# An instruction planner with measured waits, half-width prices and the exclusion of two engines

## The chip, the cores and the metric

The kernel runs on one core of a Trainium2 chip. The metric is the device time of one execution in microseconds (us). The kernel before took 1173.47 us, the median of three runs between 1171.46 and 1174.13.

## The reference

Two layers act on 1024 tokens of width 1024, in float32. Each layer normalises its input, projects it with one matrix into the inputs of four groups of heads and a gate, runs the groups, normalises each group, multiplies by the gate, projects back and adds the normalised result to its input:

```python
h = rmsnorm(x, g_pre) @ w_in
ya = swa_sink_attention(a_q, a_k, a_v, sinks)        # A: window of 128, softmax
yb = short_gated_conv(b_b, b_c, b_x, conv_w, conv_b) # B: gated convolution
yc = mla(c_q, c_kv, c_kr, pos, ...)                  # C: causal softmax, low-rank q and kv
yd = stick_breaking_attention(d_q, d_k, d_v)         # D: sigmoid breaks
y = concat of rmsnorm(group) * silu(gate)
x = x + rmsnorm(y @ w_out, g_post)
```

In group D the weight of key j for query i is sigmoid(z_ij) times the product of 1 - sigmoid(z_ik) over the keys k between them.

## The kernel before

**Engines and precision.** All large products are matmuls on TensorE (PE). A float32 operand is held as two halves, a rounded high part and the rest; most products take three matmuls (high by high, high by low, low by high). Making the halves, a *split*, takes a cast on ScalarE (ACT) for the high part and a subtraction on VectorE (DVE) or GpSimd (POOL) for the low part. Most splits read the accumulator in PSUM and run on VectorE. Those of weights read SBUF and may run on either engine.

**Tiles.** xg are the long-lived tiles (34 buffers), xw the weights' splits and also the name of the projection's two accumulator banks, xP six tiles of attention weights (128 queries by up to 1024 keys), xsc three banks of scores, xtr two banks of transposes, xpv the one bank of the values' product, xPT the split of transposed attention weights, xf tiles of the gate, xt small temporaries.

**Group D.** A task takes one head and 256 queries, as two blocks of 128. For each block the scores go through two sigmoids on ScalarE, then VectorE runs the cumulative product, a `tensor_tensor_scan` of 128 x w with w up to 1024, and a multiply of 128 x (w - 1), both in place in xP tiles. The following task step `pv_causal` transposes the blocks on TensorE into xtr, splits them into xPT (ScalarE the cast, VectorE the subtraction), and multiplies them with the values into xpv. The trace's operation TENSOR_TENSOR_SCAN is printed in the order as SCALAR_TENSOR_TENSOR of xP with xP. The four heads come as two pairs; the scores of the first pair are D0, of the second D1.

**What sets the order.** No order is written by hand. The work is a set of streams (Python generators: norms, projections, scores, value products, gates, output). A planner, the class `Weaver`, runs them while the program is built, and keeps a clock of its own: `now` for TensorE and a list of busy stretches for each of VectorE, ScalarE, GpSimd and the DMA queue. Whenever TensorE is free by that clock, `run` takes the first stream whose operands are ready by it, or else the one ready soonest. Every instruction of the other engines is issued through one call in the class `Tracked` (line 85, so all of them carry L85 in the trace). `enter` computes when an instruction's operands are ready, with a latency from the table `LAT` by the engine that made them and the engine that reads (P TensorE, V VectorE, A ScalarE, G GpSimd, D DMA, S a scan), and how long it takes; `place` puts it in the first gap of its engine that is long enough. The order on each engine is then pinned as the planner's clock has it, so it stays the same on the chip, while the instants do not: an instruction waits for its real operands. `sooner` decides between GpSimd and VectorE for the splits of weights, with 300 ns added against VectorE.

**What the change cannot alter.** The projection stream takes two banks in turn; its tiles for group A's keys wait until the last scores of D1 have been recorded. `matmul` (L479) and `transpose` (L483) carry the names xw, xsc, xpv and xtr of the bank that they fill.

## Time and profile before

| | us |
|---|---|
| median of three runs | 1173.47 |
| the profiled execution | 1172.81 |
| its span, first to last instruction | 1171.0 |
| PE busy | 1142.7 |
| DVE busy | 822.9 |
| ACT busy | 640.1 |
| POOL busy | 347.9 |

Each layer repeats the same sequence: the input norm and the projections for C and B, the attention of C, the stage of group D (255 to 400 us and 832 to 977 us of the span), then groups A, the gates and the output projection. TensorE is close to always busy, so the idle stretches of TensorE and what ended them are the first thing to read. A bracket at a row's end, [2.10 <-DVE xPT L85], is the idle time before its instructions and the instruction that ended it. PEclk is the granted clock of TensorE as a share of 2.4 GHz. Busy time of a matmul is longer than the distance between two starts, since matmuls overlap: the distance is what counts in a sum.

### The profile page before, as it was taken

What the parts mean: (1) busy time and instruction counts of PE and PEld (TensorE: products, weight loads), DVE (VectorE), ACT (ScalarE), POOL (GpSimd) and SP (SyncE); (2) the same over time, 40 slices, a digit from 0 to 9 for tenths busy, and PEclk for the clock granted to TensorE, in tenths of its full rate; (3) what the DMA queues carried; (4) which work ended last, traced back from release to release, by engine and by line L of the source; (5) the groups of instructions that cost most, each with busy time, mean ns of one, the idle gap of its engine ahead of it and who ended that gap; (6) DMA issues with size and microseconds to landing.
All of it is one profiled execution on the core that took longest, in us unless ns stands there. A gap on an engine that the chain in (4) does not pass through costs nothing.

```text
span 1171.0 us, 17883 instructions
## 1 busy us (share of the span) xinstructions
PE 1142.7 (98%) x6302; PEld 978.2 (84%) x6302; DVE 822.9 (70%) x1685; ACT 640.1 (55%) x1443; POOL 347.9 (30%) x477
## 2 busy tenths in 40 slices
PE   8999999999999999999999999999999999999997
PEld 6988888987787788878889888899878877888886
DVE  6868687549969878852764777873688788888323
ACT  7665566246556667631454655651655565675211
POOL 4225143116224235310221332420353332451000
PEclk9999999999999999999999999999999999999999
DMA  6121202121111011321451122021201111124123
GB/s 227 36 64 33 68 19 60 50 81 27 27 37 37 18 37 52 98 73 46 161 166 29 37 54 55 19 82 36 76 25 37 27 28 28 28 64 155 61 72 126
DMA packets 72678, 71.98 MB, mean 61 GB/s; under 512 B 10062, under 2 KB 59276, under 8 KB 72588
## 3 DMA queue, kind: packets, MB, share of 16 engines
q1 hardware_dynamic: 72588, 70.83, 20.4%
q8 instruction: 50, 0.82, 0.3%
q14 instruction: 40, 0.33, 0.1%
HBM read 55.09 MB, written 11.53 MB: 57 GB/s over the span
## 4 chain that ended last, share of the span: by engine, by line
PE 73%; DVE 14%; ACT 5%; issue 4%; DMA 2%; POOL 1%; SPq 0%; DVEq 0%; POOLq 0%; ACTq 0%
PE xw L479 37%; PE xsc L479 22%; PE xtr L483 8%; DVE xP L85 7%; PE xpv L479 6%; DVE xg L85 3%; ACT xP L85 2%; DMA xP<-in_w_out_dram 1%; DVE xPT L85 1%; ACT xg L85 1%; DVE xs L85 1%; ACT xt L85 1%; DVE xt L85 1%; POOL xs L85 1%; DVE xw L85 1%
## 5 line engine op out<-in xcount | busy, mean ns | idle before, releaser
L479 PE MATMUL xw<-xg,xw 128*128 128x512 f32 x2064 | 516.7, 396 | 2.4 <-DVE xf L85 2.4
L479 PEld LDWEIGHTS xw<-xg,xw 128*128 128x128 f32 x2064 | 376.0, 188 | 75.3 <-DVE xf L85 3.3
L479 PE MATMUL xsc<-xg,xg 128*128 128x512 f32 (+7 forms) x1400 | 307.2, 364 | 0.3 <-ACT xP L85 0.2
L479 PEld LDWEIGHTS xsc<-xg,xg 128*128 128x128 f32 (+1 forms) x1400 | 239.0, 190 | 37.6 <-ACT xP L85 4.1
L85 POOL TENSOR_SCALAR xP<-xP,xs 128x256 f32<-128x256 f32 (+7 forms) x128 | 82.5, 656 | 161.7 <-DVE xs L85 113.5
L85 ACT CAST xPT<-xtr 128x512 fp32r<-128x512 f32 (+1 forms) x192 | 101.2, 550 | 49.7 <-PE xtr L483 48.1
L479 PE MATMUL xpv<-xPT,xg 128*128 128x256 f32 (+1 forms) x720 | 120.2, 290 | 7.0 <-DVE xPT L85 6.5
L483 PE MATMUL xtr<-ident,xP 128*128 128x128 f32 (+1 forms) x843 | 124.3, 275 | 2.7 <-DVE xP L85 1.5
L85 DVE TENSOR_TENSOR xPT<-xtr,xPT 128x512 fp32r<-128x512 f32 (+1 forms) x192 | 117.0, 630 | 11.3 <-ACT xPT L85 10.9
L479 PEld LDWEIGHTS xpv<-xPT,xg 128*128 128x128 f32 x720 | 103.2, 189 | 23.9 <-DVE xPT L85 13.6
L479 PE MATMUL xw<-xg,xg 128*128 128x416 f32 (+2 forms) x648 | 114.5, 326 | 0.0
L85 DVE TENSOR_TENSOR xg<-xw,xg 64x512 fp32r<-64x512 f32 (+1 forms) x112 | 62.9, 574 | 69.7 <-ACT xg L85 68.5
L85 ACT CAST xg<-xw 64x512 fp32r<-64x512 f32 (+1 forms) x112 | 53.4, 492 | 103.0 <-PE xw L479 92.5
L483 PEld LDWEIGHTS xtr<-ident,xP 128*128 128x128 f32 (+1 forms) x843 | 97.7, 141 | 14.2 <-DVE xP L85 3.5
L85 ACT ACTIVATE xP<-xP,xs 128x256 f32<-128x256 f32 (+7 forms) x128 | 80.7, 631 | 49.0 <-DVE xs L85 43.8
L85 POOL TENSOR_TENSOR xw<-xraw,xw 128x512 fp32r<-128x512 f32 x42 | 64.8, 1546 | 139.2 <-ACT xw L85 102.7
L479 PEld LDWEIGHTS xw<-xg,xg 128*128 128x128 f32 x648 | 102.0, 189 | 1.9
L85 DVE TENSOR_TENSOR_SCAN xP<-xP 128x128 f32<-128x128 f32 (+3 forms) x64 | 95.3, 1488 | 4.3 <-ACT xP L85 4.2
L85 POOL TENSOR_TENSOR xt<-xt 64x128 f32<-64x128 f32 x64 | 40.0, 626 | 153.1 <-DVE xt L85 124.6
L85 ACT ACTIVATE xP<-xsc 128x512 f32<-128x512 f32 (+2 forms) x192 | 80.1, 514 | 9.2 <-DVE xP L85 8.1
L85 ACT ACTIVATE xt<-xsc 128x512 f32<-128x512 f32 x32 | 19.2, 599 | 116.4 <-PE xsc L479 92.6
L85 ACT COPY xt<-xpv 64x512 f32<-64x512 f32 x80 | 46.7, 584 | 44.7 <-PE xpv L479 43.4
(128 smaller groups left out, 1291.9 us busy)
## 6 DMA issues: line engine op xcount, KB each, us to landing
xraw<-in_w_in_dram SPq DMA_DIRECT2D x96, 256.0 KB, 2.8
xP<-in_w_out_dram SPq DMA_DIRECT2D x16, 512.0 KB, 3.9
xg<-in_x_dram SPq DMA_DIRECT2D x8, 512.0 KB, 9.0
xg<-xP SPq DMA_DIRECT2D x32, 128.0 KB, 2.3
xP<-in_x_dram SPq DMA_DIRECT2D x8, 512.0 KB, 4.2
xP<-xs SPq DMA_DIRECT2D x8, 512.0 KB, 3.8
xs<-xP SPq DMA_DIRECT2D x7, 512.0 KB, 3.5
out_dram<-xP SPq DMA_DIRECT2D x7, 512.0 KB, 2.6
```

Of the source, the lines that this page charges most:

```text
L85: ins = real(*args, **kw)
L479: in_order(T.matmul(ps, lhs, rhs, start=start, stop=stop, skip_group_check=True))
L483: in_order(T.transpose(ps, src, idn))
```

## The change

It changes the planner's prices; no line that issues work is touched.

- The table of latencies takes new numbers (ScalarE to TensorE 250 to 165 ns, VectorE to TensorE 195 to 140, VectorE to VectorE 60 to 115, GpSimd to TensorE 190 to 60, a new one of 110 for ScalarE to ScalarE, and others).
- An instruction of at most 64 partitions and at least 128 elements is priced 125 ns more on ScalarE and 95 ns more on VectorE. `tensor_reduce` is priced 117 ns more.
- The factor 1.12 on VectorE's `tensor_tensor` between SBUF operands goes; the price of GpSimd's goes from 2.5 to 2.25 ns an element.
- `place` gets a flag `pair`. It is set for VectorE's scans, its `tensor_tensor` with SBUF operands, its `tensor_scalar` with SBUF operands, and GpSimd's `tensor_tensor`, all with at least 128 elements. Such an instruction may not start by the planner's clock while one of the other engine's is running. It is not set for GpSimd's `tensor_scalar` or VectorE's `scalar_tensor_tensor`. `sooner` asks with the flag set.

```diff
 LAT = {
-    "PA": 197, "PV": 197, "AV": 90, "AP": 250, "AG": 160, "VP": 195, "VA": 128, "VG": 155,
+    "PA": 198, "PV": 200, "AV": 137, "AP": 165, "AG": 177, "VP": 140, "VA": 128, "VG": 165,
...
-    def place(self, key, t, dur, keep=True):
+    def place(self, key, t, dur, keep=True, pair=False):
         busy = self.busy[key]
-        i = len(busy)
-        while i > 0 and busy[i - 1][1] > t:
-            i -= 1
-        while i < len(busy) and busy[i][0] < t + dur:
-            t = max(t, busy[i][1])
-            i += 1
+        other = self.port["G" if key == "V" else "V"] if pair else ()
+        while True:
+            i = len(busy)
+            while i > 0 and busy[i - 1][1] > t:
+                i -= 1
+            while i < len(busy) and busy[i][0] < t + dur:
+                t = max(t, busy[i][1])
+                i += 1
+            end = max([e for s, e in other if s <= t < e], default=t)
+            if end <= t:
+                break
+            t = end
         if not keep:
             return t
+        if pair:
+            self.port[key] = self.port[key][-40:] + [(t, t + dur)]
...
+        pair = False
+        half = out.shape[0] <= 64 and n >= 128
         if key == "A":
...
+            dur += 125.0 * half
...
         elif key == "V":
-            half = op == "tensor_scalar" and not bank
-            dur = 69.0 + (0.52 if half else 1.04) * n + 62.0 * scalars
+            fast = op == "tensor_scalar" and not bank
+            dur = 69.0 + (0.52 if fast else 1.04) * n + 62.0 * scalars + 95.0 * half
+            pair = (fast or op == "tensor_tensor") and not bank and n >= 128
             if op == "tensor_tensor_scan":
                 dur = 110.0 + 2.12 * n
-            elif op == "tensor_tensor" and not bank:
-                dur *= 1.12
+                pair = True
+            elif op == "tensor_reduce":
+                dur += 117.0
...
         elif op == "tensor_scalar":
             dur = 244.0 + 0.833 * n
         else:
-            dur = 148.0 + 2.5 * n
+            dur = 148.0 + 2.25 * n
+            pair = n >= 128
...
-        t = self.place(key, t, dur)
+        t = self.place(key, t, dur, pair=pair)
...
-            dur = 148.0 + 2.5 * n if e.key == "G" else 69.0 + 1.04 * n
-            t = self.place(e.key, t, dur, False) + dur + (300.0 if e.key == "V" else 0.0)
+            dur = 148.0 + 2.25 * n if e.key == "G" else 69.0 + 1.04 * n
+            t = self.place(e.key, t, dur, False, True) + dur + (300.0 if e.key == "V" else 0.0)
```

The sets of instructions on TensorE, ScalarE and the DMA queue stay the same; three splits in all move from VectorE to GpSimd, as a balance of moves both ways. What moves is the order. Three places of the first layer follow; the second layer has the same. Numbers behind names differ between the two programs, so the same tile has two numbers.

VectorE, second head pair of D, before: the splits of a task's transposes, the scans and multiplies of the next one (blocks of 896 and 1024 keys), and at the end the task's last split, of 384 columns.

```order
L85 TENSOR_TENSOR xPT_4299<-xtr_4294,xPT_4299 128x512
L85 TENSOR_TENSOR xPT_4314<-xtr_4309,xPT_4314 128x512
L85 SCALAR_TENSOR_TENSOR xP_4302<-xP_4302 128x896
L85 TENSOR_TENSOR xP_4303<-xP_4303,xP_4302 128x895
L85 SCALAR_TENSOR_TENSOR xP_4325<-xP_4325 128x1024
L85 TENSOR_TENSOR xP_4326<-xP_4326,xP_4325 128x1023
L85 TENSOR_TENSOR xPT_4355<-xtr_4351,xPT_4355 128x384
```

The same place with the change:

```order
L85 TENSOR_TENSOR xPT_4308<-xtr_4303,xPT_4308 128x512
L85 TENSOR_TENSOR xPT_4316<-xtr_4311,xPT_4316 128x512
L85 SCALAR_TENSOR_TENSOR xP_4319<-xP_4319 128x896
L85 TENSOR_TENSOR xP_4320<-xP_4320,xP_4319 128x895
L85 TENSOR_TENSOR xPT_4358<-xtr_4354,xPT_4358 128x384
L85 SCALAR_TENSOR_TENSOR xP_4334<-xP_4334 128x1024
L85 TENSOR_TENSOR xP_4335<-xP_4335,xP_4334 128x1023
```

The split of 384 columns has moved from behind both scans to between them.

TensorE at the same place, before: six projection groups of three matmuls, the three matmuls that read that last split, and the transposes that read the two multiplied blocks.

```order
L479 MATMUL xw_4284<-xg_386,xw_4019 128x512 x3
L479 MATMUL xw_4284<-xg_387,xw_4019 128x512 x3
L479 MATMUL xw_4284<-xg_388,xw_4191 128x512 x3
L479 MATMUL xw_4284<-xg_389,xw_4191 128x512 x3
L479 MATMUL xw_4284<-xg_390,xw_4191 128x512 x3
L479 MATMUL xw_4284<-xg_391,xw_4191 128x512 x3
L479 MATMUL xpv_4346<-xPT_4355,xg_2539 128x256 x3
L483 MATMUL xtr_4404<-ident,xP_4303 128x128
L483 MATMUL xtr_4404<-ident,xP_4326 128x128
```

The same place with the change, from the fourth of what are now four groups in a row:

```order
L497 MATMUL xw_4261<-xg_395,xw_4191 128x512 x3
L497 MATMUL xpv_4349<-xPT_4358,xg_2464 128x256 x3
L497 MATMUL xsc_4406<-xg_3793,xg_3523 128x512
L497 MATMUL xsc_4406<-xg_3794,xg_3523 128x512
L497 MATMUL xsc_4411<-xg_3793,xg_3523 128x384
L497 MATMUL xsc_4411<-xg_3794,xg_3523 128x384
L497 LDWEIGHTS identb
L497 MATMUL xsc_4411<-maskD,identb 128x128
L497 MATMUL xsc_4421<-xg_3793,xg_3523 128x512
L497 MATMUL xsc_4421<-xg_3794,xg_3523 128x512
L501 MATMUL xtr_4426<-ident,xP_4320 128x128
L501 MATMUL xtr_4426<-ident,xP_4335 128x128
```

Six score matmuls of the following task now stand between the three value matmuls and the transposes; before, they stood behind the transposes.

VectorE, first head pair of D, before: two tasks' scans and multiplies (blocks of 768, then 640 and 768 keys), and behind them the product xf of a gate, which empties the projection's bank.

```order
L85 SCALAR_TENSOR_TENSOR xP_3285<-xP_3285 128x768
L85 TENSOR_TENSOR xP_3286<-xP_3286,xP_3285 128x767
L85 SCALAR_TENSOR_TENSOR xP_3317<-xP_3317 128x640
L85 TENSOR_TENSOR xP_3318<-xP_3318,xP_3317 128x639
L85 SCALAR_TENSOR_TENSOR xP_3332<-xP_3332 128x768
L85 TENSOR_TENSOR xP_3333<-xP_3333,xP_3332 128x767
L85 SCALAR_TENSOR_TENSOR xf_3367<-xf_3367,xw_3234 128x512
```

With the change, the first two scans at the place:

```order
L85 SCALAR_TENSOR_TENSOR xP_3238<-xP_3238 128x640
L85 TENSOR_TENSOR xP_3239<-xP_3239,xP_3238 128x639
L85 SCALAR_TENSOR_TENSOR xP_3253<-xP_3253 128x768
L85 TENSOR_TENSOR xP_3254<-xP_3254,xP_3253 128x767
L85 SCALAR_TENSOR_TENSOR xf_3274<-xf_3274,xw_3155 128x512
L85 TENSOR_TENSOR xPT_3287<-xtr_3282,xPT_3287 128x512
L85 TENSOR_TENSOR xPT_3294<-xtr_3290,xPT_3294 128x384
```

The gate's product now stands behind one task's two scans, of 640 and 768.

## Rows read from the trace of the kernel before

**Rows 1.** Page, busy us, share of the span and instructions of each engine.
```profile
PE 1142.7 (98%) x6302; PEld 978.2 (84%) x6302; DVE 822.9 (70%) x1685; ACT 640.1 (55%) x1443; POOL 347.9 (30%) x477
```

**Rows 2.** Windows: stretch, length, busy us (instructions) by engine, PEclk, DMA share, GB/s.
```profile
255.00:400.00 145.00, 139.78 (x747) 114.50 (x746) 121.95 (x156) 88.99 (x188) 55.63 (x49) 0.99 0.13 33
...
832.00:977.00 145.00, 139.64 (x749) 114.57 (x747) 122.07 (x156) 89.36 (x189) 55.42 (x49) 0.99 0.12 32
```

**Rows 3.** Waits of PE: line, releaser: us in total, times, longest us.
```profile
PE xpv L479 <- DVE xPT L85: 6.5, 10, 2.1
...
PE xw L479 <- DVE xf L85: 2.4, 2, 1.2
...
PE xtr L483 <- DVE xt L85: 2.3, 2, 1.2
```

**Rows 4.** Timeline of PE, first layer: start, us, instructions, [idle before <-releaser].
```profile
388.76 4.04 PE L479 MATMUL xw<-xg,xw 128*128 128x512 f32 x17
392.64 0.28 PE L479 MATMUL xpv<-xPT,xg 128*128 128x256 f32 x1
395.01 0.51 PE L479 MATMUL xpv<-xPT,xg 128*128 128x256 f32 x2 [2.10 <-DVE xPT L85]
```

**Rows 5.** Timeline of DVE, same stretch.
```profile
386.93 2.01 DVE L85 TENSOR_TENSOR_SCAN xP<-xP 128x896 f32<-128x896 f32 x1
389.05 1.09 DVE L85 TENSOR_TENSOR xP<-xP,xP 128x895 f32<-128x895 f32 x1
390.05 2.28 DVE L85 TENSOR_TENSOR_SCAN xP<-xP 128x1024 f32<-128x1024 f32 x1
392.44 2.05 DVE L85 TENSOR_TENSOR xP<-xP,xP 128x1023 f32<-128x1023 f32 x1
394.42 0.54 DVE L85 TENSOR_TENSOR xPT<-xtr,xPT 128x384 fp32r<-128x384 f32 x1
```

**Rows 6.** Timeline of POOL, same stretch.
```profile
390.86 2.55 POOL L85 TENSOR_TENSOR xw<-xraw,xw 128x512 fp32r<-128x512 f32 x1 [3.92 <-ACT xw L85]
```

**Rows 7.** Windows at this place, in both layers (columns as in rows 2).
```profile
392.92:395.01 2.09, 0.00 (x0) 0.00 (x0) 2.06 (x3) 1.70 (x3) 0.77 (x2) 1.00 0.18 35
395.01:399.24 4.23, 4.23 (x18) 3.58 (x19) 3.39 (x6) 3.07 (x6) 1.91 (x3) 0.60 0.40 107
...
971.77:976.00 4.23, 4.23 (x18) 3.60 (x19) 3.36 (x6) 3.21 (x7) 1.86 (x3) 0.60 0.38 106
```

**Rows 8.** Timeline of PE: three other waits of the first D stage.
```profile
277.38 0.98 PE L479 MATMUL xpv<-xPT,xg 128*128 128x256 f32 x6 [0.41 <-DVE xPT L85]
...
295.03 0.98 PE L479 MATMUL xw<-xg,xw 128*128 128x512 f32 x3 [1.19 <-DVE xf L85]
...
311.13 0.98 PE L483 MATMUL xtr<-ident,xP 128*128 128x128 f32 x7 [0.59 <-DVE xP L85]
```

**Rows 9.** Timeline of DVE ahead of the second of them.
```profile
290.47 2.84 DVE L85 TENSOR_TENSOR_SCAN xP<-xP 128x768 f32<-128x768 f32 x1
...
294.30 0.68 DVE L85 SCALAR_TENSOR_TENSOR xf<-xf,xw 128x512 f32<-128x512 f32 x1
```

**Rows 10.** Timeline of POOL, same stretch.
```profile
287.51 4.19 POOL L85 TENSOR_TENSOR xw<-xraw,xw 128x512 fp32r<-128x512 f32 x2
```

**Rows 11.** Timeline of DVE, a multiply with GpSimd idle beside it.
```profile
320.04 1.22 DVE L85 TENSOR_TENSOR xP<-xP,xP 128x1023 f32<-128x1023 f32 x1
```

**Rows 12.** Timeline of PE at the start.
```profile
13.96 0.66 PE L483 MATMUL xsc<-ident,xP 128*128 128x128 f32 x4 [1.94 <-DVE xP L85]
```

**Rows 13.** Window after that wait (columns as in rows 2).
```profile
13.96:20.00 6.04, 6.04 (x36) 6.01 (x37) 4.85 (x13) 5.35 (x14) 1.80 (x3) 1.00 1.06 330
```

**Rows 14.** Groups by form: engine op names shapes xcount | busy us, mean ns | idle, releasers.
```profile
L85 POOL TENSOR_TENSOR xw<-xraw,xw 128x512 fp32r<-128x512 f32 x42 | 64.8, 1546 | 139.2 <-ACT xw L85 102.7 <-issue 35.5 <-POOL xg L85 0.5
...
L85 POOL TENSOR_SCALAR xP<-xP,xs 128x256 f32<-128x256 f32 x64 | 35.4, 571 | 15.1 <-DVE xs L85 5.8 <-ACT xP L85 4.6 <-ACT xf L85 4.4
```

**Rows 15.** The same of DVE.
```profile
L85 DVE TENSOR_TENSOR xw<-xraw,xw 128x512 fp32r<-128x512 f32 x46 | 35.0, 761 | 11.5 <-ACT xw L85 9.0 <-PE xtr L483 2.4
```

More of the change, by code (lines that the diff above doesn't have):

```diff
@@ L118, in __init__ @@
         self.funcs = [(0.0, 0)]
+        self.port = {"V": [], "G": []}
         self.done = set()
@@ L276, in enter @@
         else:
-            dur = 148.0 + 2.5 * n
+            dur = 148.0 + 2.25 * n
+            pair = n >= 128
             if args[-1] == ALU.pow:
                 dur = 400.0 + 162.0 * n
-        t = self.place(key, t, dur)
+                pair = False
+        t = self.place(key, t, dur, pair=pair)
         if key == "A" and func in TABLES and func:
```

4 rows, old and new, of the table LAT are left out of this document.

## The prediction

> **What bounds the kernel now.** I read the page's busy shares first. TensorE is busy for 1142.7 us of a span of 1171.0 [rows 1], so a new order, which removes no matmul, can win only TensorE's idle time, 28.3 us, and time lost to a lower clock. The windows by stage come second: in each of the two stages of group D (255 to 400 and 832 to 977 us), TensorE misses 145.00 - 139.78 = 5.2 and 145.00 - 139.64 = 5.4 us, and VectorE is busy for 122 of 145 us, 84% [rows 2]. In these stages two engines share the bound. Third come TensorE's waits: the dearest is value matmuls xpv waiting for VectorE's xPT, 6.5 us in ten waits, the longest 2.1; then xw waiting for xf, 2.4 in two, and two waits for xt, 2.3 [rows 3].
>
> Fourth comes the place of the longest wait. TensorE runs 17 matmuls of the projection from 388.76 to 392.64, 0.228 us each, has one matmul of xpv ending at 392.92, and stands until 395.01 [rows 4]. VectorE was busy all that time [rows 7]: it ran the scan of 896, its multiply, the scan of 1024 and its multiply, and the small xPT (0.54 us) that TensorE wanted came last, at 394.42 [rows 5]. The last multiply took 2.05 us, against 1.22 for one with nothing beside it [rows 5, 11]. A GpSimd split started at 390.86, inside the scan, and ended at 393.41, inside the multiply [rows 6]. The wait has a second price. For 4.23 us behind it TensorE's granted clock is 0.60 on average, which means that most of the stretch ran at 1.2 GHz and the rest at 2.4; the second layer shows the same 0.60 over 4.23 us [rows 7]. At full clock that work is 4.23 x 0.60 = 2.54 us, so 1.69 us is lost. One such place costs 2.10 + 1.69 = 3.8 us, two layers 7.6.
>
> **The change part by part.** It changes numbers by which the planner orders instructions; the work on TensorE, ScalarE and the DMA queue is the same set. So I cost places.
>
> The place just named, in both layers. In the new order the small xPT stands ahead of the scan of 1024 and its multiply. VectorE would reach it at 390.05 and be done near 390.6, 2.3 us before TensorE needed it at 392.92 [rows 4, 5], so that wait goes. Late next is the multiply of 1023: the transposes xtr behind it read its result, and the projection's stream cannot fill the gap, because its next tiles wait until the last group of scores of this stage is recorded. What the planner does put ahead of the transposes is six score matmuls of the next task, which stood behind them before. At most they take 6 x 0.228 = 1.37 us [rows 4]. Three matmuls of xpv (half as wide, about 0.35 by the same rows) and one transpose make TensorE arrive between 394.3 and 394.8. VectorE ends the multiply at 392.44 + 2.05 = 394.49 plus the 0.5 that xPT now takes in front of it, 395.0 [rows 5]. What remains is a wait of 0.2 to 0.7; I take 0.7, since the scores also have to find their banks free. If GpSimd stays out of the way, 0.83 less of multiply, it is nothing. If it stretches the scan too by as much again, it is 1.5. Is a wait of 0.7 followed by a low clock? Behind a wait of 1.94 at the start the clock of the next 6 us is 1.00 [rows 12, 13]; so I take no clock loss. Gain: 3.8 - 0.7 = **3.1 us in each layer, 6.2 in both**, bounds 0 (the wait is only moved) and 3.8.
>
> The first head pair of the same stage. Two waits should go. At 277.38 TensorE waits 0.41 for an xPT [rows 8] that stood behind two scans; it now stands ahead of them. At 295.03 it waits 1.19 for xf, which empties a bank of the projection [rows 8]; xf ran at 294.30 behind three scans, one of them stretched to 2.84 us beside GpSimd's two splits [rows 9, 10]. It now stands behind two scans. Together 1.6. Against that, the new order sends TensorE faster into VectorE's queue: between the last scores and the next xpv there are now eight projection groups of three matmuls (24 x 0.228 = 5.5 us) and seven transposes, while VectorE owes two scans, two multiplies, xf and xPT, about 6 us at the durations of [rows 5, 9] scaled by width, and more when one is stretched. I put 1.1 of new small waits there. The wait at 311.13, 0.59 [rows 8], is a multiply of 1023 again and I leave it. Net **-0.5 in each layer, -1.0 in both**; bounds -1.6 to +1 each.
>
> The start. The wait of 1.94 [rows 12] ends with VectorE's normalisation of a block of rows, beside which GpSimd runs two splits. In the new order more of these splits are on VectorE, and one more group of three matmuls stands ahead of the wait: 3 x 0.2. I take half, **-0.3**; bounds -0.6 to +0.6.
>
> The engine choice. In total three more of the splits go to GpSimd, where one of 512 columns takes 1546 ns on average against 761 on VectorE [rows 14, 15]. GpSimd is busy for 30% of the span [rows 1] and the split weights are fetched some tiles ahead, so this is nothing as long as that lead holds; without it each costs 1546 - 761 = 0.8 us, 2.4 in all. The two waits for xt, 2.3 us [rows 3], have the same fifteen matmuls ahead of them in both orders: unchanged. The other places, with under 0.3 us each, I leave at zero, with 1.5 either way.
>
> Sum: -6.2 - 1.0 - 0.3 = -7.5 us. The profiled run took 1172.81 with a span of 1171.0, 0.66 below the median of 1173.47. It becomes 1165.3; against the median the same sum gives **1166.0**.
>
> **The rivals.** *Waits only change places.* The planner's instant of a split is not the chip's: the one at 390.86 started when ScalarE released it, in the middle of a scan [rows 6]. If one falls on the scan of 896 and another on the multiply of 1023, each adds 0.83, TensorE stands first at xpv and then at xtr, 2 us or more in sum, and the clock falls as before. The gain at the place is then nil and 1.3 is left: 1172.2, or 1173.5 if the other stage's new waits eat that also. For it: VectorE's total work in the stage does not shrink. Against it: the piece that TensorE needs first is now two long instructions earlier.
>
> *VectorE becomes the bound of the D stages, slower.* Eight projection groups in a row ahead of one xpv, in the first head pair, use up the filler that used to lie between other tasks. If VectorE's two scans and two multiplies there are stretched by 0.83 twice, xpv stands for 2 us and, being as long as the wait at 395.01, brings the same loss of 1.69: +3.8 a layer, 7.6 in both. With the gain of 6.2 it would still come out near no change; it is slower where the D1 gain fails too, 1173.5 + 7.6 - 1.6 x 2 = 1177.9, and 1181 if the two old waits stay. The point from which it decides is a wait of about 2 us at that xpv. For it: 84% of VectorE in the stage [rows 2], and the low clock after 2.10 us. Against it: the clock stayed at 1.00 after 1.94.
> The Trainium skill, "SBUF — State Buffer", section "Who interferes with whom", says that of VectorE and GpSimd the one that starts first holds the port they share for its whole instruction and the other is blocked fully; the rows of the split and the stretched multiply agree. By that rule a split that starts a little ahead of a scan holds up the whole queue on VectorE, which is this rival's trigger, and no table of durations excludes it when the starts drift. It also counts GpSimd's tensor_scalar, which the new clock leaves out of the exclusion: these take 571 ns on average for 256 columns, where the clock writes 244 + 0.833 x 256 = 457 [rows 14].
>
> *More than the sum.* Splits stay clear of scans in the whole stage: the rest wait goes (1.4), the new small waits of the first head pair as well (2.2), and the wait at 311.13 (1.2): 1166.0 - 4.8 = 1161.
>
> **How the numbers follow.** Likeliest, 1164 to 1169: 0.60. More than the sum, near 1161: 0.09. Waits change places, 1171.2 to 1174.5: 0.17. Slower, 1176 to 1181: 0.14. A measurement of this kernel tells about 0.2%, 2.3 us, from no change. The first two are faster by more than that: 0.69; same 0.17; slower 0.14. The range leaves out the slower case and the lowest part of the larger gain: 1161 to 1175. The likeliest case's own range is 1163.5 to 1169.5, from the bounds of the rest wait (0 to 1.5 a layer) and of the first head pair.
>
> **What would show it.** Right: no wait near 2 us at the xpv of the second head pair in either layer, and windows of 4 us behind it with a granted clock of 1.00; a wait of 0 to 1.5 for xP at the transposes that follow; xw waiting for xf gone from the list; the D stages some 3.6 us shorter each, the other stages within 1 us. Wrong: a granted clock near 0.60 anywhere in a D stage, a wait of 2 us at another tile, or VectorE's scans and multiplies longer in sum than before. If the time falls and the D stages do not, my reading of the place is wrong even with the right sign.

## The result, and the profile after

The changed kernel takes 1162.05 us, the median of four runs between 1160.64 and 1162.68, against 1173.71 (1171.46 to 1174.13) for the kernel before: a ratio of 0.9901, with a 95% interval of 0.9889 to 0.9913. That is 11.7 us, where 7.5 were forecast. The profiled run, the fastest of the four, took 1160.64 us with a span of 1158.8.

The page of the kernel after gives these shares of the engines. Against [rows 1], TensorE is busy for 9.4 us less with the same matmuls, since the ends of matmuls in the profile are modelled and part of the time lost between two starts counts as busy; VectorE for 7.9 us less, although it lost only three instructions; GpSimd for 2.9 us less, although it has three more.

```profile
PE 1133.3 (98%) x6302; PEld 978.0 (84%) x6302; DVE 815.0 (70%) x1682; ACT 639.7 (55%) x1443; POOL 345.0 (30%) x480
```

TensorE's waits, to be read beside [rows 3]:

```profile
PE xtr L501 <- DVE xP L85: 4.9, 3, 2.3
PE xtr L501 <- DVE xt L85: 3.7, 2, 2.2
PE xw L497 <- DVE xf L85: 2.7, 4, 0.9
...
PE xpv L497 <- DVE xPT L85: 0.3, 2, 0.2
```

Waits for xPT at the value matmuls fell from 6.5 us to 0.3. Waits for xP at the transposes are 4.9 us in three, two of them of 2.3, where the kernel before had this row:

```profile
PE xtr L483 <- DVE xP L85: 1.5, 3, 0.6
```

Waiting for xf did not go away: 2.7 us in four in place of 2.4 in two. Waiting for xt grew from 2.3 to 3.7.

The place that the prediction is about, in TensorE's timeline (start, us, instructions, idle before):

```profile
387.05 0.50 PE L497 MATMUL xpv<-xPT,xg 128*128 128x256 f32 x2 [0.17 <-DVE xPT L85]
...
391.39 0.98 PE L501 MATMUL xtr<-ident,xP 128*128 128x128 f32 x7 [2.32 <-DVE xP L85]
```

VectorE there, and behind it GpSimd:

```profile
382.39 2.02 DVE L85 TENSOR_TENSOR_SCAN xP<-xP 128x896 f32<-128x896 f32 x1 [0.53 <-ACT xP L85]
384.51 2.02 DVE L85 TENSOR_TENSOR xP<-xP,xP 128x895 f32<-128x895 f32 x1
386.45 0.55 DVE L85 TENSOR_TENSOR xPT<-xtr,xPT 128x384 fp32r<-128x384 f32 x1
386.92 2.27 DVE L85 TENSOR_TENSOR_SCAN xP<-xP 128x1024 f32<-128x1024 f32 x1
389.30 2.03 DVE L85 TENSOR_TENSOR xP<-xP,xP 128x1023 f32<-128x1023 f32 x1
```

```profile
384.29 1.29 POOL L85 TENSOR_TENSOR xw<-xraw,xw 128x512 fp32r<-128x512 f32 x1 [2.50 <-ACT xw L85]
388.71 1.54 POOL L85 TENSOR_TENSOR xw<-xraw,xw 128x512 fp32r<-128x512 f32 x1 [3.12 <-ACT xw L85]
```

The small xPT runs between the two scans, as the order has it, and the wait at the value matmuls shrank from 2.10 us [rows 4] to 0.17. A few score matmuls later TensorE stands for 2.32 us for the second multiply. Both multiplies took 2.0 us, against 1.09 and 1.22 undisturbed [rows 5, 11]: a GpSimd split runs beside each (a *collision* in what follows). The second layer shows the same, with a wait of 2.33 us.

In the profiled run it is the granted clock behind this wait that changed. The windows (length, busy us by engine, PEclk) behind the wait in layer one, in layer two, and behind a wait of 2.17 us at 1065:

```profile
391.39:395.60 4.21, 4.21 (x23) 3.41 (x24) 4.11 (x5) 3.68 (x8) 1.81 (x1) 1.00 0.24 64
...
960.97:965.00 4.03, 4.03 (x22) 3.27 (x23) 3.95 (x5) 3.68 (x8) 1.63 (x1) 1.00 0.24 63
...
1065.61:1069.90 4.29, 4.29 (x14) 3.58 (x15) 2.80 (x5) 1.38 (x3) 2.60 (x2) 0.60 0.53 163
```

It is 1.00 twice, where [rows 7] had 0.60 twice, although the wait is longer. At 1065 it is 0.60.

That is one run of the four. The mean granted clock over the span is on record for each: 0.998 in the profiled one, 0.996 in the other three, which have no trace to show where it fell. Taken as (1 - clock) x span, 2.2 us are lost in the profiled run, 0.5 of them in the tail behind the last matmuls, and about 4.6 (4.1 at least, by the rounding) in each of the others. No trace here loses more than 2.2 in the tail, so by this estimate the others lost more than the one low clock that the profiled run shows. The profiled run of the kernel before loses 5.4 us, 2.0 of them in the tail; its runs beside the experiments have means of 0.9954 to 0.9965, which is 4.1 to 5.4. Between the medians the clock can thus give some 1 us, and most of the 11.7 is order.

### Where the 12.2 us of the span went

To compare kernels stage by stage, I take the distance between the starts of each two successive matmuls or transposes on TensorE, less the usual distance of the first one's shape (227 ns for 512 columns, 173 for 384, 118 for 256, 108 for a transpose), and add these up. A stage ends when the same number of projection matmuls has been issued as in the kernel before, so that it holds nearly the same work. The warm-up on zeros at the start with the first small transpose behind it, 4.8 us before and 5.7 after, is left out. All in us, from one profiled execution each; C1 and C2 are the stages up to the start of D in the two layers, A1 and A2 those behind D.

| kernel | C1 | D1 | A1 | C2 | D2 | A2 | sum |
|---|---|---|---|---|---|---|---|
| before | 11.4 | 13.9 | 4.8 | 7.0 | 13.9 | 4.1 | 55.0 |
| changed | 7.7 | 9.7 | 4.8 | 4.0 | 9.7 | 6.1 | 41.9 |

The sum falls by 13.1, the warm-up takes 0.9 more: 12.2, the difference of the spans. Each D stage gains 4.2, each C stage 3.0 to 3.7, A2 loses 2.0. Sorted by size over the whole program, steps that lose over 1 us sum to 11.95 before and 12.11 after: nothing was won there. Steps of 0.15 to 1 us went from 16.0 to 9.2, shorter ones from 23.7 to 19.1, and time lost at the low clock from 3.3 to 1.5 (the tail apart); the last of these is of the two profiled runs.

### The profile page after: what moved, and what is told of

It is laid out like the page before. It is cut to its first block, busy times and chain, and to the rows that moved or that the text cites. A ratio compares the mean times of both kernels' runs of the same rounds, so it can differ in the third digit from the quotient of the medians.

```text
span 1158.8 us, 17859 instructions
## 1 busy us (share of the span) xinstructions
PE 1133.3 (98%) x6302; PEld 978.0 (84%) x6302; DVE 815.0 (70%) x1682; ACT 639.7 (55%) x1443; POOL 345.0 (30%) x480
## 5 line engine op out<-in xcount | busy, mean ns | idle before, releaser
L85 DVE TENSOR_TENSOR xPT<-xtr,xPT 128x512 fp32r<-128x512 f32 (+1 forms) x192 | 116.3, 629 | 13.1 <-ACT xPT L85 12.6
L497 PE MATMUL xpv<-xPT,xg 128*128 128x256 f32 (+1 forms) x720 | 114.9, 286 | 0.4 <-DVE xPT L85 0.3
L85 POOL TENSOR_TENSOR xw<-xraw,xw 128x512 fp32r<-128x512 f32 x47 | 68.4, 1458 | 138.9 <-ACT xw L85 106.5
L85 DVE TENSOR_TENSOR_SCAN xP<-xP 128x128 f32<-128x128 f32 (+3 forms) x64 | 90.5, 1414 | 3.0 <-ACT xP L85 2.7
L85 ACT ACTIVATE xt<-xsc 128x512 f32<-128x512 f32 x32 | 19.1, 598 | 113.2 <-PE xsc L497 89.3
```

What stands on the lines that cost most here:

```text
L85: ins = real(*args, **kw)
L497: in_order(T.matmul(ps, lhs, rhs, start=start, stop=stop, skip_group_check=True))
```

## The experiments: which part of the change does it

Three ingredients can be told apart: the latencies (L), the durations (D: 64 partitions, the reduce, the factor 1.12, GpSimd's 2.25 ns) and the exclusion in `place` (X).

**e1_lat, the latencies alone.** Only the table differs from the kernel before:

```diff
-    "PA": 197, "PV": 197, "AV": 90, "AP": 250, "AG": 160, "VP": 195, "VA": 128, "VG": 155,
+    "PA": 198, "PV": 200, "AV": 137, "AP": 165, "AG": 177, "VP": 140, "VA": 128, "VG": 165,
...
```

> The kernel before with the new table of latencies alone; durations and the placing of GpSimd against VectorE as before. In its order the small xPT at the second head pair of D still stands behind both scans, as before. Theory A (the gain of 11.7 us has three parts: about 7 from small waits of the C stages, by the latencies; 3.3 from the low clock behind the 2.1 us wait in both layers, by the swap of the small xPT; the rest in the first head pair): this kernel gives the part of the C stages, 1166 to 1168, and keeps a granted clock near 0.60 behind a wait of 2.1 us in both layers. Rival B (the latencies matter little, the C stages gain from prices of durations and from the exclusion): 1171 to 1174. Rival C (the whole change is needed, parts undo one another): slower than before, over 1176.

Measured 0.9989 (0.9980 to 0.9999), 1.3 us. C2 is 6.8, after 7.0 in the kernel before. Theory A falls: the latencies by themselves are worth almost nothing. In the profiled run the low clock stays with the old order, as A had it; TensorE's wait, and the window behind it:

```profile
396.25 0.50 PE L479 MATMUL xpv<-xPT,xg 128*128 128x256 f32 x2 [2.10 <-DVE xPT L85]
```

```profile
396.25:400.48 4.23, 4.23 (x18) 3.59 (x19) 3.38 (x6) 3.21 (x7) 1.88 (x3) 0.60 0.40 108
```

It does not fall behind both waits in every run, though: six of the ten runs have a mean clock of 0.998 or 0.999, at most 2.9 us lost, where two such windows (3.41 us at half the clock each) alone would cost 3.4.

**e2_excl, the exclusion alone.**

```diff
-        t = self.place(key, t, dur)
+        t = self.place(key, t, dur, pair=pair)
...
-            t = self.place(e.key, t, dur, False) + dur + (300.0 if e.key == "V" else 0.0)
+            t = self.place(e.key, t, dur, False, True) + dur + (300.0 if e.key == "V" else 0.0)
```

> The kernel before with the exclusion alone: VectorE and GpSimd instructions that share SBUF operands are kept apart in the plan, old latencies and durations. Its order has the small xPT between the two scans. Theory A: the low clock of 3.4 us is gone in both layers, 3.3 us, and VectorE's instructions are stretched less; C stages as before: 1168 to 1171. Rival B: part of the C stages too, 1164 to 1167. Rival C: over 1174.

Measured 0.9998 (0.9988 to 1.0008), no difference. The table below shows why: the D stages gain 4.8 and 4.2, as with the whole change, and the A stages lose 6.4 and 5.6. The losses stand in TensorE's timeline of group A, where scores wait for the statistics of the softmax, with the clock at 1.2 GHz in part of what follows (0.70 on average from 428.79 to 440.00, some 3.4 us of the loss in A1):

```profile
428.79 0.74 PE L496 MATMUL xsc<-xg,xg 128*128 128x256 f32 x4 [0.96 <-DVE xs L85]
431.14 1.55 PE L496 MATMUL xsc<-xg,xg 128*128 128x256 f32 x8 [1.61 <-DVE xs L85]
```

At the second head pair the swap is there, and the wait with it, now at a score matmul whose bank ScalarE has to empty:

```profile
392.90 0.73 PE L496 MATMUL xsc<-xg,xg 128*128 128x512 f32 x2 [1.74 <-ACT xP L85]
```

**e3_dur, the durations alone**, and **e4_noexcl, latencies and durations without the exclusion.** e3 differs from the kernel before by

```diff
+            dur += 125.0 * half
...
+            dur = 69.0 + (0.52 if fast else 1.04) * n + 62.0 * scalars + 95.0 * half
...
-            elif op == "tensor_tensor" and not bank:
-                dur *= 1.12
+            elif op == "tensor_reduce":
+                dur += 117.0
...
-            dur = 148.0 + 2.5 * n
+            dur = 148.0 + 2.25 * n
```

and e4 from the changed kernel by

```diff
-        t = self.place(key, t, dur, pair=pair)
+        t = self.place(key, t, dur)
...
```

> The kernel before with the new durations alone (64 partitions dearer, the reduce dearer, no factor 1.12, GpSimd 2.25 ns an element), old latencies, no exclusion. Its order has the small xPT between the scans, and ten more splits on GpSimd than before. Theory A: low clock gone, C stages as before: 1168 to 1171. Rival B: part of the C stages, 1164 to 1167. Rival C: over 1174.

> The change without the exclusion: new latencies and durations. If the exclusion does little on the chip, since instants drift away from the plan (in the changed kernel a split of GpSimd still lies across both long multiplies at the second head pair): 1161 to 1164. If keeping the two engines apart is what makes the waits shorter: 1166 to 1170, with VectorE's scans and multiplies longer in sum than in the changed kernel.

Measured: e3 0.9933 (0.9909 to 0.9957), 7.9 us; e4 0.9945 (0.9927 to 0.9963), 6.5 us. The durations carry most of the gain, and without the exclusion 5 us of it are missing, up to 2 of them perhaps by the clock (a mean of 0.9948 over the four runs of e4, 0.9965 over those of the changed kernel). What the exclusion does is seen on VectorE: the 64 scans and 64 multiplies of group D take 155.1 us in sum in the kernel before, 155.9 in e3 and 156.1 in e4, against 150.5 in the changed kernel and 148.4 in e2. The plan takes 5 to 7 us of stretch off VectorE over the program, though not at the second head pair. Both e3 and e4 have the swapped order and the wait of 2.3 us at the transposes. In e3 the two layers stand there for the same time, 2.31 and 2.33 us, and the windows behind show that the clock fell in one of them only:

```profile
392.13:396.40 4.27, 4.27 (x16) 3.32 (x17) 4.12 (x5) 3.78 (x8) 1.86 (x1) 0.60 0.23 59
967.61:971.80 4.19, 4.19 (x23) 3.44 (x24) 4.11 (x5) 3.68 (x8) 1.78 (x1) 1.00 0.24 61
```

**e7_half, the price of 64 partitions alone.**

```diff
+        small = out.shape[0] <= 64 and n >= 128
...
+            dur += 125.0 * small
...
-            dur = 69.0 + (0.52 if half else 1.04) * n + 62.0 * scalars
+            dur = 69.0 + (0.52 if half else 1.04) * n + 62.0 * scalars + 95.0 * small
```

> The kernel before with one price changed: instructions of at most 64 partitions 125 ns dearer on ScalarE and 95 ns on VectorE. Theory A (this price is what the durations' gain of 8 us comes from, since 80 splits, 80 casts and 80 copies of 64x512 are behind the plan by it): 1165 to 1168. Rival (the gain comes from the other terms, the factor 1.12 and GpSimd's 2.25): 1171 to 1176.

Measured 0.9971 (0.9958 to 0.9983), 3.4 us: in time part of the durations' gain, less than theory A had. Its profile has five windows of low clock besides the tail's, 7.9 us lost against 3.3 before. Nine of its ten runs have a mean clock of 0.992 to 0.994; the tenth, with 0.998, took 1166.25 us, about what e3 takes at that clock (1165.35). By that single run the price of 64 partitions alone may make most of the durations' order, as theory A had it, with the clock taking the gain back; this is not shown.

**e8_oldlat, durations and exclusion, old latencies.** Against the changed kernel:

```diff
-    "PA": 198, "PV": 200, "AV": 137, "AP": 165, "AG": 177, "VP": 140, "VA": 128, "VG": 165,
+    "PA": 197, "PV": 197, "AV": 90, "AP": 250, "AG": 160, "VP": 195, "VA": 128, "VG": 155,
...
```

> The change with the old table of latencies (new durations and the exclusion). The latencies alone gave 1.1 us. If they add the same here: 1163 to 1164. If they are worth more beside right durations, since ready times are sums of both: 1165 to 1168. If the exclusion without them is harmful: over 1168.

Measured 0.9899 (0.9876 to 0.9922): the whole change without its latencies is as fast as with them. In the profiles the stages are a balance. Wherever latencies and durations are both new (the change, e4, e9, e10, e12), C2 is 3.9 to 4.4; with new durations and old latencies (e3, e8, e11) it is 6.3 each time. The A stages go the other way: 7.6 us for both in e8, 10.9 in the changed kernel, but 1.65 of that is the one low clock in A2 of its profile.

| kernel | ratio to before | C1 | D1 | A1 | C2 | D2 | A2 | sum |
|---|---|---|---|---|---|---|---|---|
| e1: L | 0.9989 | 11.8 | 13.8 | 5.0 | 6.8 | 14.3 | 4.6 | 56.3 |
| e2: X | 0.9998 | 10.3 | 9.1 | 11.2 | 7.0 | 9.7 | 9.7 | 57.0 |
| e3: D | 0.9933 | 7.6 | 11.1 | 6.7 | 6.3 | 10.8 | 5.2 | 47.7 |
| e4: L, D | 0.9945 | 10.3 | 11.6 | 7.2 | 3.9 | 11.6 | 6.4 | 51.0 |
| e8: D, X | 0.9899 | 8.0 | 9.7 | 4.0 | 6.3 | 9.7 | 3.6 | 41.3 |
| changed: L, D, X | 0.9901 | 7.7 | 9.7 | 4.8 | 4.0 | 9.7 | 6.1 | 41.9 |
| e7: 64 partitions | 0.9971 | 9.5 | 11.7 | 8.3 | 5.0 | 11.2 | 8.4 | 54.1 |

## The experiments: the wait, the clock and the collisions

**e5_fill, the clock by itself.** The kernel before, with zeros multiplied while TensorE would stand:

```diff
                 diag = j == t0
+                if diag and task["kind"] == "D" and task["h"] == 3 and t0 == 4:
+                    fill(8)
```

> The kernel before, in the same order on every engine, with eight matmuls of zeros (128x512, bf16) put on TensorE ahead of the three value matmuls that wait 2.1 us at the second head pair of D, in both layers. They fill about 1.8 us of the wait and delay nothing. Theory A (the low clock is the price of TensorE standing still): no window of 0.60 behind the wait in either layer, the wait for xPT shrinks by the filling alone, and the time falls by 2 x 1.65 = 3.3 us, to about 0.997 of before. Rival (the clock falls there for another cause): 0.60 stays behind the place, time within 0.1% of before.

At the place it does what theory A says; TensorE's timeline (7 of the 8 filling matmuls are in the trace) and the window behind:

```profile
393.89 1.90 PE L492 MATMUL xfill<-idle 128*128 128x512 bf16 x7
...
396.27 0.51 PE L479 MATMUL xpv<-xPT,xg 128*128 128x256 f32 x2 [0.36 <-DVE xPT L85]
```

```profile
396.27:400.50 4.23, 4.21 (x29) 3.61 (x30) 3.98 (x7) 3.67 (x8) 1.91 (x3) 1.00 0.43 110
```

The clock is 1.00 in both layers, and each D stage is 1.4 us shorter. The time is shorter by less than the runs can tell: 0.9994 (0.9981 to 1.0006), where theory A had 0.997. In the profiled run C1 is 1.0 us worse, with a window of low clock at 10 us that the kernel before does not have, and A1 0.8 worse, where the wait for xt grew to 2.0 us. So 2.8 us won in the D stages of the profile came out as some 0.7 in the medians, and 2.2 at most by the interval. That the loss at the start has anything to do with the filling is not shown. The clocks on record agree with the small gain: a mean of 0.9965 over the 19 runs of the kernel before beside it and 0.9973 over the ten runs of e5, which is 0.9 us. The kernel before does not pay for two low clocks in each of its runs: four of the 19 have 0.998.

**e6_nosplit, the collisions taken away.** The changed kernel in the same order; the low half of the weights split by GpSimd between the last scores of the two head pairs is left at zero, so no GpSimd split reads SBUF there:

```diff
+            if e is G and on:
+                W.enter("G", "tensor_tensor", sub, {})
+                W.behind("G", nc.gpsimd.memset(f(t[:, 1, :m]), 0.0).ins)
```

> The changed kernel, in the same order on every engine, with GpSimd's splits of weights between the last scores of D0 and those of D1 replaced by a memset, which reads nothing: the low half of these weights is left at zero. Theory A (the 2.3 us wait for the last multiply is made by two such splits, each of which stretches a multiply by 0.8 to 0.9 us): both multiplies go to 1.1 and 1.2 us, the wait to 0.5 to 0.8 in both layers, the time falls by 3 to 3.5 us against the changed kernel (0.987 of before). Rival (VectorE's work in the stage sets the end, the collisions are hidden): the wait only moves to another tile of the stage, under 1 us gained.

Measured 0.9826 (0.9812 to 0.9841), 0.0075 below the changed kernel's ratio, some 8.8 us, where 3 to 3.5 were expected. VectorE's two multiplies are at their undisturbed length, and TensorE's longest wait for xP is 1.0 us:

```profile
384.68 1.09 DVE L85 TENSOR_TENSOR xP<-xP,xP 128x895 f32<-128x895 f32 x1
...
388.54 1.22 DVE L85 TENSOR_TENSOR xP<-xP,xP 128x1023 f32<-128x1023 f32 x1
```

```profile
PE xtr L501 <- DVE xP L85: 2.3, 3, 1.0
```

The D stages give 2.9 us each (9.7 to 6.8), which is 5.7 of the 8.8; the profiled runs show spans 5.2 us apart (1158.8 and 1153.6), and the medians differ by more because the changed kernel's profiled run is the fastest of its four and that of e6 the slowest. Up to 2 us of the 8.8 may be clock: a mean of 0.9983 over the four runs of e6 against 0.9965. More than half of the wait at the transposes, 1.3 of 2.3 us, is made by collisions, and the plan's exclusion does not keep them off.

**e9_pinG and e10_pinGV, the exclusion kept on the chip.** Same order on every engine as the changed kernel. In e9 each GpSimd subtraction also waits, by a semaphore, for the last VectorE instruction of the pair that is planned to end before it starts; in e10 VectorE waits for GpSimd in the same way as well. `KEEP` is "G" in e9 and "GV" in e10.

```diff
+        if pair:
+            if key in KEEP:
+                old = [s for s in self.port["G" if key == "V" else "V"] if s[1] <= t and s[2]]
+                self.held = max(old, key=lambda s: s[1])[2].name if old else None
...
+        if self.held:
+            self.tc.add_manual_dep(
+                ins, self.held,
+                mybir.DependencyInfo(mybir.DependencyClass.Sync, mybir.DependencyReason.DATA),
...
```

> The changed kernel, in the same order on every engine; each GpSimd subtraction of at least 128 columns also waits for the VectorE instruction that shares its operands' side in the plan and is planned to end before it. Theory A (the exclusion in the plan is lost on the chip because GpSimd starts a split as soon as its operands are there, ahead of its planned place): VectorE's multiplies of the second head pair lose part of the 0.8 to 0.9 us of stretch, the D stages get 1 to 3 us shorter each, 1156 to 1160. Rival (late splits hold up the weights, or fall on the next scan all the same): 1161 to 1166, with TensorE waiting for GpSimd's splits.

> As e9_pinG, and VectorE's instructions of the pair also wait for the GpSimd instruction planned to end before them, so that the plan's exclusion is kept from both sides. Theory A with VectorE at its bound: VectorE now waits for splits that come late, and the gain of the other side is lost: 1160 to 1166. Rival (both sides kept apart is what the plan's times assume, and all stretch goes): under 1157, with the VectorE multiplies of 895 and 1023 at 1.1 and 1.2 us.

e9: 1155.09 us, 0.9826 (0.9807 to 0.9845), faster than the changed kernel by as much as leaving the work out; up to 2.9 us of that may be clock (a mean of 0.999 over its four runs), and whether the shorter waits hold it up is not shown. VectorE and GpSimd at the place, then TensorE's waits for xP:

```profile
384.29 1.09 DVE L88 TENSOR_TENSOR xP<-xP,xP 128x895 f32<-128x895 f32 x1
...
385.77 2.91 DVE L88 TENSOR_TENSOR_SCAN xP<-xP 128x1024 f32<-128x1024 f32 x1
388.78 1.22 DVE L88 TENSOR_TENSOR xP<-xP,xP 128x1023 f32<-128x1023 f32 x1
```

```profile
384.32 2.21 POOL L88 TENSOR_TENSOR xw<-xraw,xw 128x512 fp32r<-128x512 f32 x1 [2.75 <-ACT xw L88]
390.23 1.28 POOL L88 TENSOR_TENSOR xw<-xraw,xw 128x512 fp32r<-128x512 f32 x1 [3.71 <-ACT xP L88]
```

```profile
PE xtr L516 <- DVE xP L88: 3.8, 4, 1.6
```

The first split now starts 0.03 us behind the multiply of 895, where in the changed kernel it started 0.22 us ahead of it (384.29 against 384.51). The multiply runs in 1.09 us, and it is the split that is stretched, to 2.21. It then meets the scan of 1024, which takes 2.91 us in place of 2.27. The second split starts at 390.23, behind the multiply of 1023, which runs in 1.22. In the changed kernel it had started at 388.71, half a microsecond before the end of the scan, and so ahead of the multiply. The wait goes from 2.3 to 1.6 us and each D stage from 9.7 to 7.7; VectorE's scans and multiplies take 145.1 us in sum, after 150.5.

e10: 0.9934 (0.9912 to 0.9955), 0.0033 above the change, at the edge of the two intervals, and 0.0108 above e9. The stretch is gone, as the rival had it (139.9 us for the scans and multiplies in sum), and the time is lost all the same: VectorE is made to wait for splits that come late, and TensorE for VectorE:

```profile
PE xw L512 <- DVE xf L88: 5.6, 4, 1.9
PE xtr L516 <- DVE xP L88: 4.3, 4, 1.9
```

**e11_pinG_oldlat, e9 with the old latencies** (the diff of e8_oldlat, on e9_pinG).

> e9_pinG with the old table of latencies. Theory A (the latencies are worth nothing once durations and the exclusion are in, as e8_oldlat showed without the waits): within 0.3% of e9_pinG, 1152 to 1158. Rival (they matter when the plan's exclusion is kept): over 1158.

Measured 0.9851 (0.9834 to 0.9867), 2.9 us above e9, though in other runs and with intervals that overlap: no clear difference, as without the waits.

**e12_pinG_wide, more kinds kept apart.**

```diff
-            pair = (fast or op == "tensor_tensor") and not bank and n >= 128
+            pair = (fast or op in ("tensor_tensor", "scalar_tensor_tensor")) and not bank and n >= 128
...
             dur = 244.0 + 0.833 * n
+            pair = n >= 128
```

> e9_pinG with two more kinds of instruction kept apart in the plan and by the wait: GpSimd's tensor_scalar of at least 128 columns and VectorE's scalar_tensor_tensor with SBUF operands. Theory A (they exclude one another too; the stretch of GpSimd's tensor_scalar of 256 columns, 571 ns on average before, goes to about 0.48, and the C and A stages get up to 2 us shorter each): 1150 to 1154. Rival (these stretches lie beside TensorE's work and the new order costs as much as it brings): 1154 to 1160.

Measured 1148.8 us, 0.9782 (0.9768 to 0.9797), below what theory A had and the fastest here: 25.8 us below the kernel before and a further 1.2% below the change. Its page:

```profile
PE 1129.6 (98%) x6302; PEld 977.1 (85%) x6302; DVE 804.5 (70%) x1680; ACT 638.7 (56%) x1443; POOL 350.0 (31%) x482
```

The kind that was added, of 256 columns, in the changed kernel and in e12 (instructions, busy us, mean ns):

```profile
L85 POOL TENSOR_SCALAR xP<-xP,xs 128x256 f32<-128x256 f32 x64 | 34.3, 554 | 26.7 <-ACT xw L85 14.7 <-DVE xs L85 5.2 <-ACT xf L85 3.5
```

```profile
L88 POOL TENSOR_SCALAR xP<-xP,xs 128x256 f32<-128x256 f32 x64 | 32.5, 526 | 25.4 <-ACT xw L88 14.7 <-DVE xs L88 5.9 <-ACT xP L88 2.5
```

It gets 28 ns shorter on average, to 526 and not to the 480 that theory A had, and the D stages are where e9 has them. The gain is in A1 and A2, 2.3 and 1.8 after 4.5 and 4.1 in e9, where TensorE's waits for xt are gone from the list, and in C1, where e9's profile has a low clock that e12's has not. Whether the exclusion of the added kinds did it, or the other order that follows from it, this run does not separate. The last table, for these kernels:

| kernel | ratio to before | C1 | D1 | A1 | C2 | D2 | A2 | sum |
|---|---|---|---|---|---|---|---|---|
| e5 (fill counted as work) | 0.9994 | 12.4 | 10.9 | 5.6 | 7.1 | 10.9 | 4.3 | 51.3 |
| e6 | 0.9826 | 9.0 | 6.8 | 4.9 | 3.9 | 6.8 | 5.3 | 36.8 |
| e9 | 0.9826 | 8.2 | 7.7 | 4.5 | 4.2 | 7.6 | 4.1 | 36.4 |
| e10 | 0.9934 | 7.1 | 12.0 | 6.3 | 4.3 | 12.3 | 5.8 | 47.6 |
| e11 | 0.9851 | 7.3 | 7.6 | 4.8 | 6.3 | 7.6 | 3.5 | 37.1 |
| e12 | 0.9782 | 6.1 | 7.7 | 2.3 | 4.4 | 7.6 | 1.8 | 29.8 |

## Why the prediction held, and which of its steps did not

The sign and the range (1161 to 1175) held, near its lower end; the likeliest case, 1164 to 1169, did not. The working behind the number did not hold up as well, and that the time still fell inside the range is in good part luck: what was forecast at the second head pair did not come, and stages that were left at zero made up for it. Of the signs that the prediction named as wrong, a wait of 2 us at another tile was there (2.32 at xtr); of those that it named as right, the wait for xP of at most 1.5, the wait for xf gone and the other stages within 1 us failed.

- **The second head pair, forecast -3.1 a layer.** The wait at the value matmuls went, as forecast. "What remains is a wait of 0.2 to 0.7; I take 0.7" is the step that failed: 2.32 us remained, 2.49 with the 0.17 ahead, more than the 2.10 before. In the profiled run the place gained some 1.5 us a layer, all of it clock. Two quantities were off. From the start of the scan of 896 to the end of the second multiply I had 386.93 to 395.0, 8.1 us; it took 382.39 to 391.33, 8.9, because a split met the first multiply too (2.02 for 1.09). And TensorE had 6.5 us of work from the start of that scan (382.39 to 389.07, less the wait of 0.17), where I reckoned 7.5 from the old trace: VectorE's scan began 0.53 us late, behind a sigmoid of ScalarE, and the rest is the new order ahead of the place, which I had not followed. e6 shows what the wait is without collisions: 1.0 us.
- **The low clock, 1.69 a layer of that sum.** Its price was about right (the stage sums give 1.65, e5 1.4). Its condition was not: I tied it to a wait of some 2 us. The wait stayed and the clock did not fall in the profiled run, in either layer. So the gain at the place in that run is a gain of clock alone, and by e3 not one that must recur; in the other three, with a mean clock of 0.996, more was lost. The argument from the wait of 1.94 at the start, behind which the clock stayed at 1.00, does not hold either: in the profiles of e4 and e7 the same wait, 1.93 and 1.95 us, was followed by a low clock within 0.6 us.
- **"Waits only change places".** This rival, with 0.17, described what happened at its place. It was wrong about the time, since it took the low clock along and the rest as unchanged.
- **The first head pair, forecast -0.5.** The whole D stage was forecast 3.6 shorter and is 4.2: 1.65 of clock, 0.1 in the steps over 1 us, 1.4 in those of 0.15 to 1 us, 1.1 in shorter ones. The wait for xPT at 277 went; the one for xf only shrank, from 1.19 to 0.89, and a second one came (2.7 us in four waits over both layers). Near in size, by other terms.
- **"The other places ... I leave at zero, with 1.5 either way".** The largest miss: C1 gave 3.7 and C2 3.0. Of C1's, 1.1 is the wait at the start (2.1 to 1.04; forecast 0.3). The rest is waits of under 0.7 us, which I had put at nothing since none of them stood out. A planner's prices act everywhere at once, and nearly half of the gain came from where no single row was worth a sentence. By e1, e3 and e8 the whole gain of C2 needs the durations and the latencies together; part of it came with one price alone (5.0 in e7).
- **The waits for xt, "the same fifteen matmuls ahead of them in both orders: unchanged".** They went from 2.3 to 3.7 us, and one brought a low clock: A2 lost 2.0. The order was the same, but ScalarE's copy out of xpv stands behind a cast that waits for a transfer, so the time of the transfer sets it, while TensorE arrives earlier: ScalarE waits 2.91 us for the transfer, and 2.20 in the kernel before. ScalarE's rows after, its cast before, and TensorE's wait after:

```profile
1062.22 0.62 ACT L85 CAST xw<-xP 128x512 fp32r<-128x512 f32 x1 [2.91 <-DMA xP<-in_w_out_dram]
1062.87 0.58 ACT L85 COPY xt<-xpv 64x512 f32<-64x512 f32 x1
```

```profile
1075.07 0.62 ACT L85 CAST xw<-xP 128x512 fp32r<-128x512 f32 x1 [2.20 <-DMA xP<-in_w_out_dram]
```

```profile
1065.61 1.11 PE L501 MATMUL xtr<-ident,xt 128*128 128x128 f32 x4 [2.17 <-DVE xt L85]
```

- **The engine choice, forecast nothing.** No run separates it. GpSimd's busy time fell.
- **The rule weighed beside the slower rival.** The Trainium skill, "SBUF — State Buffer", section "Who interferes with whom" says that whichever starts first blocks the other. e6 and e9 agree: at the multiply of 895 a start 0.22 us ahead or 0.03 us behind decides which of the two is stretched. The rule stood in the prediction as the trigger of the slower rival and as the reason why starts that drift undo the plan. This was the largest thing left in the D stages: in e9, holding the start of GpSimd's splits by a semaphore, in an unchanged order, took 2.0 us off each D stage. The same section counts any GpSimd instruction that reads SBUF, against any of VectorE with two SBUF inputs, and so the two kinds that e12 adds; e12 is the fastest, but it changes the order too, so it does not show this.

The slower rival (a wait of 2 us at the xpv of the first head pair) did not occur.

## What to carry to other kernels

When a change alters the prices of a planner, the sum over a few long waits misses half of it: here the steps over 1 us kept their sum, and the gain was in shorter ones and, in the profiled run, in the clock. Look at the granted clock of every run before a gain of clock in one profile is counted. Follow a wait to the next instruction that the same engine owes before counting it as won, with the work of both engines taken from the new order. And a plan that keeps two engines apart holds only as long as the starts do: an instruction that may start early needs a semaphore on the side that can afford to wait (GpSimd, 30% busy: 8.8 us faster in e9), and not also on the side that is close to the bound (VectorE in e10, which lost most of it again).

## What the runs showed of the hardware that was not expected

- The granted clock does not follow from the length of the wait alone. In the profiles of the kernels here there are 19 stretches of 2.0 to 2.4 us in which TensorE stood (the start apart); at 10 of them the clock fell to 1.2 GHz within 1 us of their end, for 3.4 us; at 2, both in e7, it fell 1.2 and 1.8 us behind, and at 7 not at all. Behind 2.10 and 2.12 it fell four times of four (the kernel before and e1), behind 2.31 to 2.33 five times of ten. The runs of one kernel differ as well: e1's have mean clocks from 0.995 to 0.999. What decides is open.
- A GpSimd split that starts beside a scan or a multiply of VectorE and ahead of it costs VectorE 0.64 to 0.93 us here (2.91 for 2.27 in e9, 2.02 for 1.09 in the changed kernel). Where the multiply starts first, by 0.03 us in e9 and in e10, it keeps its 1.09 us and GpSimd pays 0.9 us (2.21 and 2.22 for 1.28).
